# Long convolution by a 64 x 64 transform: sums and differences of n2 and n2+32, products on 64 x 64 quarters, the output inverse with the spectrum stationary

## The chip, the cores and the metric

One core of one Trainium2 chip. The time is that of the device in microseconds, of one execution of the program; shown are the median of three runs and one more execution taken with the profiler. All arithmetic is float32 or split into float32r parts.

## The reference

One encoder layer is applied to two request groups (g = 0, 1) of 2048 tokens and 1024 channels with the same weights:

```
h = rmsnorm(x);  p = h @ w_in                       # 1024 -> 3328 columns
y_hy = x0 * fftconv(v * x1, k2, skip) * silu(z_hy)  # 512 channels
y_cf = conformer(glu(a)) * silu(z_cf)               # 256 channels, 31 taps, LayerNorm
y_xa = attention(q, memory) * silu(z_xa)            # 256 channels, 4 heads, 256 memory tokens
y = rmsnorm(x + concat(y_hy, y_cf, y_xa) @ w_out)
```

`fftconv` is a two-sided long convolution on a circle of 4096 positions, with a filter k2 that a small network computes for each position and channel. The change lies in how this convolution is computed.

## The kernel before, in words

The transform over 4096 positions m = 64 n1 + n2 is done in two steps of 64: over n1 (to a frequency index t of 0 to 63), and over n2. The two request groups are the real and imaginary parts of one complex sequence. Values pass through DRAM between the steps.

The program has four stages:

- **Stage 1** (lines 204 to 707): the projections, 24 TensorE matmuls of 512 columns for each block of 128 output columns and 512 tokens (`proj`, L439 to L441, high and low parts). Beside them run lists of background tasks, some after every block (`background`, L653): the conformer's taps on VectorE (L235), the filter (`filter_background`, L287), and, at the end, the first eight steps of stage A (`a_background`, L613). The filter makes taps for two n2 at a time (`taps`, L330); four quarter products (L355, 64 rows by 64 columns of the array each) transform a pair over n1, two ScalarE copies (L357) evict them, and SyncE stores them to XF (L358). The gated product u = v * x1 is stored to UU for each of 4 channel blocks and 2 groups (L495).
- **Stage A** (`stage_a`, L812, 24 of 32 steps here): for two n2, the input is transposed, split, multiplied by a twiddled table (`times_t1`, L185, six matmuls in row halves), and evicted by one VectorE and one ScalarE copy to X1 (L825 to L828). Two steps go with each block of the memory attention (`attention`, L756, 16 blocks).
- **Stage B** (`stage_b`, L890): for each t of 0 to 32 the filter's row XF[t] is transformed over n2 (`spectrum`, L845: one 128 x 128 product, evicted as two tiles kr and ki of which each half stands twice), then X1[t] and, with a reversed table, X1[64-t] go through `unit` (L831): a 128 x 128 product over n2, two half copies on ScalarE that swap real and imaginary parts, two products with kr and ki, their sum on POOL, the inverse product over n2, an eviction, and a store to AA. Every third t from 9 loads and splits a block of w_out (`wo_load`, L855). The last two blocks of attention each have two steps of stage B behind them; the other steps follow.
- **Output** (lines 922 to 980): for two n2 (128 tokens), AA is loaded, two 64-column products with the table t4 invert over t (L949), ScalarE evicts (L951), four transposes turn channels to partitions (L954), VectorE multiplies by the gate from GG (L958), and 48 float32r matmuls (L972 to L974) multiply by w_out; then residual, norm and store.

A planner orders the instructions of each engine when the program is built, by its own estimate of durations; each engine then executes in that fixed order. DMA issues are instructions of the queue that issues them: loads of stage B and output on SyncE, stores to AA and of the output on ScalarE. A float32 matmul is two instructions on TensorE, a float32r matmul and a transpose one.

Buffers in stages A and B: PSUM `ms` 2, `tr` 3, `pa` 2, `po` 1 banks; SBUF tiles `in` 8, `o` 5, `us` 4, `z` 4, `k0` and `k1` 3 each.

## Time and profile before

| | us |
|---|---|
| median of three runs | 2113.95 (2110.22 to 2114.83) |
| the profiled execution's own time | 2119.94 |
| span from its first to its last instruction | 2118.2 |
| TensorE busy | 1982.9 |
| VectorE, ScalarE, POOL busy | 1262.6, 759.2, 890.4 |

In the profile PE is TensorE, PEld its weight loads, DVE VectorE, ACT ScalarE, SP SyncE; a q behind an engine's name (SPq, ACTq) is its instruction queue, where DMA issues stand. A busy share is an average over the stages, which have different limits; a matmul is pipelined, so the cadence of starts says more than the length of one. A wait is put down to what came last before the instruction started.

### The profile page before, as it was taken

To read this page: it belongs to the slowest core of one execution; us is meant where nothing else is said; L and a number is where in the kernel's file an instruction comes from. 1 tells how busy PE (TensorE), PEld (TensorE's weight loads), DVE (VectorE), ACT (ScalarE), POOL (GpSimd) and SP (SyncE) were. 2 spreads that over 40 slices of the span, in tenths; PEclk is the share of its full clock that TensorE was granted. 3 is DMA by queue.
4 is the path that set the end of the run, shared out by engine and by line. 5 is a ranking of instruction groups with operands and counts; after the bars stand their busy time and mean duration, and the time that the engine had idled before them with its cause. 6 is when DMAs were issued, how large, how long until landed. Compare 5 with 4: busy or idle time off the path is not lost. (4 is left out here: it accounts for less than half of the span.)

```text
span 2118.2 us, 26007 instructions
## 1 busy us (share of the span) xinstructions
PE 1982.9 (94%) x8866; PEld 1499.7 (71%) x8866; DVE 1262.6 (60%) x1779; ACT 759.2 (36%) x1461; POOL 890.4 (42%) x854
## 2 busy tenths in 40 slices
PE   5999988898999999999989999999988889999998
PEld 5888877776777777777767778777533267777776
DVE  4766397979325365488889622178887624434443
ACT  5531122231424233321323421278787722222221
POOL 3433576755533211466645531166588711111110
PEclk8999999999999999999999999999999999999999
DMA  9643323332557423232422235698888785555552
GB/s 335 209 145 130 94 87 96 120 119 80 203 182 220 137 89 115 81 95 65 124 69 94 87 107 173 221 288 269 246 264 257 235 219 140 147 155 151 154 144 60
DMA packets 238558, 328.72 MB, mean 155 GB/s; under 512 B 87177, under 2 KB 117913, under 8 KB 236634
## 3 DMA queue, kind: packets, MB, share of 16 engines
q1 hardware_dynamic: 146026, 260.72, 38.7%
q10 hardware_dynamic: 87056, 54.57, 9.6%
q0 software_dynamic: 5344, 11.77, 2.1%
q8 instruction: 71, 1.16, 0.2%
q14 instruction: 61, 0.50, 0.1%
HBM read 196.37 MB, written 130.61 MB: 154 GB/s over the span
## 5 line engine op out<-in xcount | busy, mean ns | idle before, releaser
L439 PE MATMUL pj<-xh,whi 128*128 128x512 f32 (+1 forms) x1728 | 671.1, 389 | 32.1 <-ACT big L505 9.3
L440 PE MATMUL pj<-xl,whi 128*128 128x512 f32 (+1 forms) x1728 | 670.1, 388 | 8.6 <-POOL xl L410 6.6
L441 PE MATMUL pj<-xh,wlo 128*128 128x512 f32 (+1 forms) x1728 | 668.7, 387 | 0.0
L235 DVE SCALAR_TENSOR_TENSOR bg<-bg,vb,bg 128x512 f32<-128x512 f32 x480 | 415.3, 899 | 11.4 <-POOL bg L230 7.0
L439 PEld LDWEIGHTS pj<-xh,whi 128*128 128x128 f32 x1728 | 331.6, 192 | 101.5 <-ACT big L505 11.0
L440 PEld LDWEIGHTS pj<-xl,whi 128*128 128x128 f32 x1728 | 332.1, 192 | 74.2 <-POOL xl L410 7.5
L441 PEld LDWEIGHTS pj<-xh,wlo 128*128 128x128 f32 x1728 | 332.0, 192 | 66.3 <-issue 2.2
L972 PE MATMUL ms<-wo,mh 128*128 128x512 f32 x512 | 204.2, 399 | 2.2 <-ACT mh L193 2.2
L973 PE MATMUL ms<-wo,mh 128*128 128x512 f32 x512 | 201.3, 393 | 0.0
L974 PE MATMUL ms<-wo,ml 128*128 128x512 f32 x512 | 194.3, 397 | 0.2 <-POOL ml L194 0.2
L462 DVE SCALAR_TENSOR_TENSOR sm<-sm,va,sm 128x448 f32<-128x448 f32 (+1 forms) x96 | 84.2, 877 | 162.4 <-POOL sm L460 143.0
L460 POOL TENSOR_SCALAR sm<-sm,va 128x448 f32<-128x448 f32 (+1 forms) x96 | 119.9, 1249 | 120.0 <-ACT sm L453 112.7
L481 POOL TENSOR_TENSOR big<-big,sm 128x448 f32<-128x448 f32 (+1 forms) x64 | 121.7, 1904 | 112.1 <-DVE sm L464 108.7
L975 DVE TENSOR_TENSOR xr<-xr,ms 128x512 f32<-128x512 f32 x64 | 44.0, 688 | 199.2 <-PE ms L974 199.0
L200 POOL TENSOR_TENSOR ss<-ss,mhalf 128x1 f32<-128x1 f32 x32 | 17.7, 553 | 313.3 <-DVE ss L199 313.3
L453 ACT COPY sm<-pj 128x512 f32<-128x512 f32 x96 | 56.2, 586 | 222.0 <-PE pj L441 189.6
L972 PEld LDWEIGHTS ms<-wo,mh 128*128 128x128 f32 x512 | 96.9, 189 | 47.5 <-issue 24.3
L974 PEld LDWEIGHTS ms<-wo,ml 128*128 128x128 f32 x512 | 96.6, 189 | 20.9 <-DVE mf L958 0.8
L973 PEld LDWEIGHTS ms<-wo,mh 128*128 128x128 f32 x512 | 96.9, 189 | 20.0
L194 POOL TENSOR_TENSOR wlo<-sm,whi 128x512 fp32r<-128x512 f32 x50 | 79.5, 1603 | 63.2 <-ACT whi L193 37.0
L198 ACT ACTIVATE junk<-xr 128x1024 bf16<-128x1024 f32 x32 | 33.8, 1058 | 191.4 <-DVE xr L975 191.4
L840 POOL TENSOR_TENSOR z<-z,us 128x512 f32<-128x512 f32 x64 | 81.9, 1289 | 28.0 <-DVE us L839 21.9
(174 smaller groups left out, 2784.2 us busy)
## 6 DMA issues: line engine op xcount, KB each, us to landing
big<-in_xt_dram SPq DMA_DIRECT2D x32, 512.0 KB, 5.4
in<-x1d SPq DMA_DIRECT2D x128, 128.0 KB, 3.9
aa<-o ACTq DMA_DIRECT2D x64, 256.0 KB, 3.6
at<-aa SPq DMA_DIRECT2D x64, 256.0 KB, 5.1
out_dram<-xr ACTq DMA_DIRECT2D x64, 256.0 KB, 3.7
sm<-in_win_dram SPq DMA_DIRECT2D x52, 256.0 KB, 3.2
ws<-whi SPq DMA_DIRECT2D x52, 256.0 KB, 2.3
ws<-wlo SPq DMA_DIRECT2D x52, 256.0 KB, 2.2
```

Source lines behind the costliest of these rows:

```text
L194: (sub_eng or nc.gpsimd).tensor_tensor(lo, src, hi.bitcast(F32), op=ALU.subtract)
L235: nc.vector.scalar_tensor_tensor(st["a", c], st["h", c][:, k:k + TB], vb[:, 2 * k + c:2 * k + c + 1], st["a", c], op0=ALU.mult, op1=ALU.add)
L439: nc.tensor.matmul(ps[:, ts_], hi, xh[:, k, ts_], start=k == 0, stop=False)
L440: nc.tensor.matmul(ps[:, ts_], hi, xl[:, k, ts_], start=False, stop=False)
L441: nc.tensor.matmul(ps[:, ts_], lo, xh[:, k, ts_], start=False, stop=k == KC - 1)
L460: nc.gpsimd.tensor_scalar(ct[:, o:e], pt[:, o + 1:e + 1], w[1], va[:, 52 + ch:53 + ch], op0=ALU.mult, op1=ALU.add)
L462: nc.vector.scalar_tensor_tensor(ct[:, o:e], pt[:, o:e], w[0], ct[:, o:e], op0=ALU.mult, op1=ALU.add)
L481: nc.gpsimd.tensor_tensor(v, v, out, op=ALU.mult)
L840: nc.gpsimd.tensor_tensor(z, z, us, op=op)
L972: nc.tensor.matmul(po, mh[:, k, :], woh[k][:, hs], start=i == 0, stop=False)
L973: nc.tensor.matmul(po, mh[:, k, :], wol[k][:, hs], start=False, stop=False)
L974: nc.tensor.matmul(po, ml[:, k, :], woh[k][:, hs], start=False, stop=i == 7)
```

## The change

The 64 values of n2 are put in the order 0, 32, 1, 33, ... so that a pair is n2 and n2+32. Where a pair is evicted (filter, `a_background`, `stage_a`), `butterfly` stores its sum and its difference: ScalarE evicts one bank, VectorE adds and subtracts. The transform over n2 then falls into one over 32 sums (even frequencies) and one over 32 differences (odd frequencies), each with real and imaginary part a 64 x 64 table, so that four such products fill the four quarters of the array.

`stage_b` takes t and 64-t together in 32 steps (t = 0 with 32): one group of four quarters transforms both, two groups make the spectrum kr and ki for both (for t = 0 four full products with a table `sk`), VectorE makes four products of them, and two groups, accumulated in PSUM, make the inverse, whose tables carry the combination of real and imaginary products. Two ScalarE copies fill one tile, and two stores of 64 rows of 4 KB go to AA. Six loads of 128 KB and two stores of 256 KB per step, as before for a pair.

The output inverse multiplies with AA's tile as the stationary operand and the table t4 (now 128 columns, for both tokens of a pair) as the moving one, eight products of 128 columns; the result has channels on partitions already. Its 128 tokens are those of n2 = n and n+32. The gate's loads become four of 64 elements a row for two of 128; the gate's product is one VectorE instruction for two. The store to UU is issued in two halves.

```diff
@@ butterfly, new; filter_background @@
+    def butterfly(a, b, px):
+        nc.scalar.copy(b, px[1])
+        nc.vector.tensor_tensor(a, px[0], b, op=ALU.add)
+        nc.vector.tensor_tensor(b, px[0], b, op=ALU.subtract)
...
+                butterfly(st["f", 0], st["f", 1], px)
                 for q in range(2):
-                    nc.scalar.copy(st["f", q], px[q])
                     nc.sync.dma_start(XF[n2p // 2, q * P:(q + 1) * P, :], st["f", q])
@@ hy_u @@
-                    nc.scalar.dma_start(UU[i].rearrange("c (n g t) -> c n g t", g=2, t=32)[:, :, g, :],
-                                        st["u"].rearrange("p (n t) -> p n t", t=32))
+                    for q in range(2):
+                        nc.scalar.dma_start(UU[i].rearrange("c (n q g t) -> c n q g t", q=2, g=2, t=32)[:, :, q, g, :],
+                                            st["u"][:, q * 1024:(q + 1) * 1024].rearrange("p (n t) -> p n t", t=32))
@@ stages A and B: psum, tiles, stage_a (a_background alike) @@
-        ms, tr, pa, po_ = psum(c2, ms=2, tr=3, pa=2, po=1)
+        ms, tr, pa = psum(c2, ms=2, tr=4, pa=2)
...
-            return tl_("in", 8)
+            return tl_("in", 7)
...
-            return tl_("o", 5)
+            return tl_("y", 2)
...
-            o = po_()
+            o = tr()
...
             times_t1(px, th, tl, uh, ul)
+            xo = tl_("z", 6), tl_("z", 6)
+            butterfly(*xo, px)
             for s in range(2):
-                xo = tl_("us", 4)
-                (nc.scalar.copy if s else nc.vector.tensor_copy)(xo, px[s])
-                nc.scalar.dma_start(X1[2 * n + s, 0:128, :], xo)
+                nc.scalar.dma_start(X1[2 * n + s, 0:128, :], xo[s])
@@ stage_b; unit, spectrum, fetch and stage_b of before are gone @@
+        lo_, hi_ = slice(0, 64), slice(64, 128)
+        def quarters(banks, jobs):
+            n = len(jobs[0][3])
+            for j in range(n):
+                for b, c, r, ops in jobs:
+                    w, x = ops[j]
+                    nc.tensor.matmul(banks[b][c, :], w[r, :], x[r, :], start=j == 0, stop=j == n - 1)
+        def spectrum(t):
+            xf = t_in()
...
+            for j in range(2):
+                pk = ms(), ms()
...
+                    w = stab[:, 2 + j, :]
+                    quarters(pk, [(0, lo_, lo_, [(w, xf)]), (0, hi_, lo_, [(w, xf)]),
+                                  (1, lo_, hi_, [(w, xf)]), (1, hi_, hi_, [(w, xf)])])
+                for b in range(2):
+                    ks.append(tl_("k", 6))
+                    nc.scalar.copy(ks[-1], pk[b])
+            return ks[0:2], ks[2:4]
...
+        def stage_b(t):
+            t1_ = 64 - t if t else 32
+            xa, xb = fetch(t, (0, 1)), fetch(t1_, (1, 0))
+            u = tr(), tr()
+            w0, w1 = stab[:, 0, :], stab[:, 1, :]
+            quarters(u, [(0, lo_, lo_, [(w0, xa)]), (0, hi_, lo_, [(w1, xb)]),
+                         (1, hi_, hi_, [(w0, xa)]), (1, lo_, hi_, [(w1, xb)])])
+            kr, ki = spectrum(t)
+            z = [[None, None], [None, None]]
+            for j, k in enumerate((kr, ki)):
+                for b in range(2):
+                    z[j][b] = tl_("z", 6)
+                    nc.vector.tensor_tensor(z[j][b], u[b], k[b], op=ALU.mult)
+            o = pa(), pa()
+            quarters(o, [(h, c, r, [(stab[:, 4 + 2 * v + j, :], z[j][b]) for j in range(2)])
+                         for h, c, r, v, b in ((0, lo_, lo_, 0, 0), (0, hi_, lo_, 1, 1),
+                                               (1, lo_, hi_, 0, 1), (1, hi_, hi_, 1, 0))])
+            om = tl_("o", 2, 1024)
+            for h in range(2):
+                nc.scalar.copy(om[:, h * TB:(h + 1) * TB], o[h])
+            for k, r in ((t, lo_), (t1_, hi_)):
+                nc.scalar.dma_start(AA[k, 0:64, :], om[r, :])
+            if t >= 9 and t % 3 == 0:
+                wo_load(t // 3 - 3)
@@ output @@
-        ms, tr = psum(c3, ms=4, tr=4)
+        ms, tr = psum(c3, ms=5, tr=3)
...
                 for g in range(2):
-                    nc.sync.dma_start(g8[:, :, g, :], chans(GG, g, n))
+                    for q in range(2):
+                        nc.sync.dma_start(g8[:, :, g, q, :], chans(GG, g, q, n))
...
-            yt = tr()
-            for s in range(2):
-                nc.tensor.matmul(yt[64 * s:64 * s + 64, :], t4[:, 2 * i + s, :], at[:, s, :], start=True, stop=True)
-            ys = sp.tile([P, TB], F32, tag="ys", name=nm("ys"))
-            nc.scalar.copy(ys, yt)
             yc = tr()
             for k in range(4):
-                nc.tensor.transpose(yc[:, k * P:(k + 1) * P], ys[:, k * P:(k + 1) * P], ident)
+                for h in range(2):
+                    nc.tensor.matmul(yc[:, k * P:(k + 1) * P], at[:, h, k * P:(k + 1) * P], t4[:, i, h, :],
+                                     start=h == 0, stop=h == 1)
```

## Rows read from the trace of the kernel before

**Rows 1.** The page, busy time, share and instructions; VectorE's busy tenths in 40 slices.

```profile
PE 1982.9 (94%) x8866; PEld 1499.7 (71%) x8866; DVE 1262.6 (60%) x1779; ACT 759.2 (36%) x1461; POOL 890.4 (42%) x854
...
DVE  4766397979325365488889622178887624434443
```

**Rows 2.** Busy us (instructions) by stage: PE, PEld, DVE, ACT, POOL; clock, DMA share, GB/s.

```profile
930.00:1200.00 270.00, 247.74 (x1060) 189.31 (x1059) 229.74 (x295) 83.11 (x118) 147.09 (x144) 0.99 0.29 86
...
1400.00:1490.00 90.00, 90.00 (x676) 64.41 (x676) 73.59 (x149) 71.63 (x237) 54.99 (x69) 1.00 0.84 264
...
1530.00:1694.00 164.00, 141.03 (x289) 51.92 (x287) 122.90 (x172) 125.05 (x219) 134.54 (x105) 0.96 0.80 254
...
1710.00:2000.00 290.00, 289.51 (x1278) 218.30 (x1279) 113.81 (x160) 64.94 (x116) 42.35 (x46) 0.99 0.60 157
```

**Rows 3.** The same, a stretch of 30 us in stage 1.

```profile
960.00:990.00 30.00, 26.57 (x116) 21.40 (x116) 30.00 (x41) 4.70 (x8) 16.02 (x16) 1.00 0.34 73
```

**Rows 4.** Groups by line, whole run: busy us, mean ns | idle before, releasers.

```profile
L840 POOL TENSOR_TENSOR z<-z,us 128x512 f32<-128x512 f32 x64 | 81.9, 1289 | 28.0 <-DVE us L839 21.9 <-DVE z L838 1.6 <-PE ms L847 1.5
...
L838 DVE TENSOR_TENSOR z<-tr,k 128x512 f32<-128x512 f32 x64 | 43.9, 689 | 23.2 <-ACT us L836 17.1 <-POOL z L840 2.7 <-issue 1.3
...
L842 PEld LDWEIGHTS pa<-z,stab 128*128 128x128 f32 x128 | 23.1, 196 | 46.1 <-POOL z L840 28.6 <-issue 15.8 <-POOL us L839 0.9
```

**Rows 5.** Line 357: duration ns min/median/max, first and last start.

```profile
L357 ACT COPY f<-ms x32: 564/589/595, 775.1 to 1236.7; 128x512 f32<-128x512 f32 x32
```

**Rows 6.** Waits, 900 to 1200 us: us in total, times, longest.

```profile
ACT f L357 <- PE ms L355: 25.8, 5, 7.5
...
PEld ms L355 <- DVE f L341: 10.5, 10, 2.5
...
ACT L340 <- DMA xf<-f: 6.2, 4, 3.2
```

**Rows 7.** Line 828, the stores of stage A: duration ns, first and last start.

```profile
L828 ACTq DMA_DIRECT2D x1d<-us x48: 326/326/1031, 1389.2 to 1491.6; - x48
```

**Rows 8.** DMA, 1530 to 1690 us: the sum, and the stores to AA with landing time.

```profile
DMA packets 23461, 41.20 MB, mean 258 GB/s; under 512 B 3737, under 2 KB 3737, under 8 KB 23336
...
aa<-o ACTq DMA_DIRECT2D x58, 256.0 KB, 3.5
```

**Rows 9.** Timeline of PE in stage B: start us, us, instruction, count.

```profile
1601.10 0.59 PE L842 MATMUL pa<-z,stab 128*128 128x512 f32 x1
1601.53 1.88 PE L833 MATMUL tr<-in,stab 128*128 128x512 f32 x4
```

**Rows 10.** Timeline of PE and PEld around one group of four quarter products.

```profile
784.26 0.21 PEld L355 LDWEIGHTS ms<-f,f 64*64 64x64 f32 x8 [0.35 <-issue]
784.26 1.09 PE L355 MATMUL ms<-f,f 64*64 64x512 f32 x8
...
785.28 0.48 PE L310 MATMUL ms<-f,wf 66*128 66x256 f32 x1
```

**Rows 11.** Timeline of PE in the output, from before L949 to after it.

```profile
1901.34 0.39 PE L974 MATMUL ms<-wo,ml 128*128 128x512 f32 x1
...
1903.00 0.39 PE L973 MATMUL ms<-wo,mh 128*128 128x512 f32 x1
```

**Rows 12.** Timeline of PE in the output, around the transposes.

```profile
1908.69 0.39 PE L973 MATMUL ms<-wo,mh 128*128 128x512 f32 x1
1908.92 0.39 PE L974 MATMUL ms<-wo,ml 128*128 128x512 f32 x1
...
1909.82 0.40 PE L972 MATMUL ms<-wo,mh 128*128 128x512 f32 x1
```

**Rows 13.** Timeline of PE in stage 1, around products of 128 columns.

```profile
66.05 0.61 PE L388 MATMUL ms<-bg,ones 128*128 128x128 f32 x4
66.41 0.36 PE L439 MATMUL pj<-xh,whi 128*128 128x256 f32 x1
66.61 0.28 PE L440 MATMUL pj<-xl,whi 128*128 128x256 f32 x1
```

More of the change, by code (lines that the diff above doesn't have):

```diff
@@ L94, in _tables, with forward @@
-    fr = (4 * np.arange(16)[:, None, None] + np.arange(2)[None, :, None] + 2 * np.arange(2)).reshape(-1)
-    fr = np.concatenate([fr, 64 + fr])
-    sf = s2(cp, sp)[fr]
-    kz, kh = kz[fr], kh[fr]
-    stab = np.stack([s2(cp, sp), s2(cpr, spr), s3(cp.T, sp.T), s3(cpr.T, spr.T), kz, kh, sf], axis=1)
+    jj, ab, pair = np.arange(32), np.arange(32)[:, None], np.arange(2)
+    def forward(k2, conj=1.0):
+        th = 2 * np.pi * ((ab * k2[None, :]) % 64) / 64
+        w = np.zeros((32, 2, 2, 32))
+        w[:, 0, 0], w[:, 1, 0] = np.cos(th), np.sin(th)
+        w[:, 0, 1], w[:, 1, 1] = -conj * np.sin(th), conj * np.cos(th)
+        return w.reshape(64, 64)
@@ new lines, in inverse, with both @@
+    def inverse(k2, conj, turned):
+        th = 2 * np.pi * ((k2[:, None] * ab.T) % 64) / 64
+        w = np.zeros((2, 32, 2, 32))
+        re = np.stack([np.cos(th), np.sin(th)], axis=1)
+        im = conj * np.stack([-np.sin(th), np.cos(th)], axis=1)
+        w[0], w[1] = (im, -re) if turned else (re, im)
+        return w.reshape(64, 64)
+    def both(a, b):
+        return np.concatenate([a, b], axis=0)
+    ev, od, evr, odr = 2 * jj, 2 * jj + 1, 62 - 2 * jj, 63 - 2 * jj
+    fk = both(forward(ev), forward(od))
@@ new lines, in _tables @@
+    kr, ki = np.tile(fk[:, :32], 2), np.tile(fk[:, 32:], 2)
+    stab = np.stack([both(forward(ev), forward(od)), both(forward(odr, -1.0), forward(evr, -1.0)), kr, ki] + [
+        both(inverse(ev, 1.0, u), inverse(od, 1.0, u)) for u in (False, True)] + [
+        both(inverse(evr, -1.0, u), inverse(odr, -1.0, u)) for u in (False, True)], axis=1)
+    sk = np.zeros((2, 32, 2, 4, 2, 2, 32))
+    for h in range(2):
+        k2 = 2 * jj + h
+        th, al = 2 * np.pi * ab * k2 / 64, np.pi * ab / 64 + 2 * np.pi * ab * k2 / 64
+        sg = (-1.0) ** h
+        g0, g1 = (np.cos(al), -np.sin(al)), (-sg * np.sin(al), -sg * np.cos(al))
+        for c_ in range(2):
+            for v in range(2):
+                sk[h, :, 0, 2 * c_ + h, h, v] = (np.cos(th), -np.sin(th))[c_]
+                sk[0, :, 1, 2 * c_ + h, 1 - h, v] = (g0[c_] + g1[c_]) / 2
+                sk[1, :, 1, 2 * c_ + h, 1 - h, v] = (g0[c_] - g1[c_]) / 2
@@ L131 @@
     X1 = dram.tile([64, 129, 512], F32, name="x1d")
-    AA = dram.tile([64, 129, 512], F32, name="aa")
+    AA = dram.tile([64, 65, 1024], F32, name="aa")
     const = ctx.enter_context(tc.tile_pool(name="const", bufs=1))
@@ L824, in stage_a @@
             times_t1(px, th, tl, uh, ul)
+            xo = tl_("z", 6), tl_("z", 6)
+            butterfly(*xo, px)
             for s in range(2):
[L826 to L843 removed]
@@ L845, in spectrum @@
-        def spectrum(x, t):
-            pk = ms()
-            nc.tensor.matmul(pk, stab[:, t, :], x, start=True, stop=True)
-            kr, ki = tl_("k0", 3), tl_("k1", 3)
-            nc.vector.tensor_copy(kr[0:64, :], pk[0:64, :])
-            nc.vector.tensor_copy(kr[64:128, :], pk[0:64, :])
-            nc.scalar.activation(ki[0:64, :], pk[64:128, :], AF.Copy, scale=-1.0)
-            nc.vector.tensor_copy(ki[64:128, :], pk[64:128, :])
-            return kr, ki
+                nc.scalar.dma_start(X1[2 * n + s, 0:128, :], xo[s])
@@ new lines @@
+        lo_, hi_ = slice(0, 64), slice(64, 128)
[7 more added lines that the diff above has]
+            xf = t_in()
+            src = XF[:, 0:256, :].rearrange("m (h e k) c -> m h e k c", h=2, e=4)
+            for h, r in enumerate((lo_, hi_)):
+                nc.sync.dma_start(xf[r, :], src[:, h, :, t, :])
+            if t == 0:
+                sk = t_in().rearrange("p (j c) -> p j c", j=4)
+                nc.sync.dma_start(sk, a["sk"])
+            ks = []
+            for j in range(2):
+                pk = ms(), ms()
+                if t == 0:
+                    for b in range(2):
+                        nc.tensor.matmul(pk[b], sk[:, 2 * j + b, :], xf, start=True, stop=True)
+                else:
+                    w = stab[:, 2 + j, :]
[5 more added lines that the diff above has]
+            return ks[0:2], ks[2:4]
@@ new lines, in fetch @@
+        def fetch(t, order):
+            x = t_in()
+            src = X1[:, 0:128, :].rearrange("(n h) (r k) c -> n h r k c", h=2, r=2)
+            for h, r in zip(order, (lo_, hi_)):
+                nc.sync.dma_start(x[r, :], src[:, h, :, t, :])
+            return x
+        def stage_b(t):
[8 more added lines that the diff above has]
+            for j, k in enumerate((kr, ki)):
+                for b in range(2):
+                    z[j][b] = tl_("z", 6)
[5 more added lines that the diff above has]
+            om = tl_("o", 2, 1024)
+            for h in range(2):
+                nc.scalar.copy(om[:, h * TB:(h + 1) * TB], o[h])
[3 more added lines that the diff above has]
+                wo_load(t // 3 - 3)
@@ L886, in more_a @@
                     na += 1
[L888 removed]
+        stab = sp.tile([P, 8, 64], F32, name="stab", bufs=1)
         nc.sync.dma_start(stab, a["stab"])
[L890 to L902 removed]
         na, nb = LEAD, 0
```

100 lines of the change are left out of this document (26 added, 74 removed).

## The prediction

> **What bounds the kernel now.** I read the page first, for engine shares and slices; then busy time by stage, since the change works in four stages with different limits; then the waits, the groups by line, and the timeline where a price had to be read off. TensorE is busy for 94% of the span, VectorE for 60%, but VectorE comes in stretches at nine tenths [rows 1]. By stage [rows 2]: in 930 to 1200 us (projections with the filter and the conformer taps beside them) TensorE still has 22 us without work, while VectorE is busy for 230 of 270 us; one 30 us stretch of it is full, 30.00 of 30 [rows 3], and two like it stand at 1050 and 1140. In 1400 to 1490 (attention with stage A) TensorE has no gap and VectorE is at 82%. In 1530 to 1694 (stage B) four engines lie between 75% and 86% and the DMA share is 0.80: no single resource, but a round of work over all of them. In 1710 to 2000 (output) only TensorE counts, 289.5 of 290.
>
> **Stage 1, the filter's pairs.** Of a pair of taps two ScalarE evictions stood after the four quarter products; now it is one eviction, a VectorE sum and a VectorE difference. The price is that of a product that reads one PSUM and one SBUF operand, 0.69 us [rows 4]: 16 pairs put 22 us on VectorE and take 16 x 0.59 = 9 us off ScalarE [rows 5]. Pairs come at about one in 29 us (32 evictions from 775 to 1237 [rows 5]), so some 9 fall into 930 to 1200, 9 x 1.38 = 13 us. Its free time there is 40 us, but not in the full stretches, where what it runs late TensorE waits for (the quarter products on the taps' product, 10.5 us) [rows 6]. A wait is added too: the sum on VectorE now waits for the eviction, which already waits for TensorE in its own order (25.8 us in 5 times) [rows 6]; queued behind it on VectorE are the conformer taps and the short convolutions, and behind those the release of SBUF for TensorE's evictions. SyncE's store of the pair goes out some 1.4 us later, and ScalarE's next exponential, which waits for that store (6.2 us now) [rows 6], a little longer. Bounds: 0 (all in free time) and +13 (all in full stretches). I take **+5**. The eight pairs of stage A at the end of stage 1 and the second DMA issue of each of the eight stores of the gated product cost nothing: VectorE and ScalarE are mostly idle after 1200, and ScalarE's evictions there wait for TensorE.
>
> **Stage A beside attention.** 24 times one more VectorE operation of 0.69 us: 16.6 us, with ScalarE's count unchanged. 48 stores, so 24 steps, start between 1389.2 and 1491.6 [rows 7]: 4.45 us a step, 8.9 us a block of attention with two of them. VectorE is busy for 73.6 of 90 us, 0.82 x 8.9 = 7.3 per block, and goes to 7.3 + 1.4 = 8.7: it fits barely. If VectorE holds no more than nine tenths of its time, the block is 9.7 us, and twelve blocks cost +9. Bounds 0 and +12 (one us a block, for sums that come late to the X1 stores); I take **+4**, nearer the sum that fits. The second buffer for the silu(z) tile instead of five is enough: its load has a whole block to land. SBUF and PSUM regroupings otherwise cost nothing: the counts per block stay.
>
> **Stage B.** Before, a frequency pair took 5.52 us: 58 stores in the 160 us from 1530, two per pair [rows 8], so 29 pairs there. Removed per pair: four half-tile copies and a negation on ScalarE, three copies and a VectorE product, and all of POOL's work (two combinations of 1.29 us and a product), for which the weight loads of the last product waited 28.6 us [rows 4]. Added: four evictions of the spectrum on ScalarE and four VectorE products of 0.69. So VectorE falls to 2.8 us per pair, POOL to the split of w_out alone, ScalarE to six evictions, 3.5 us, with two DMA issues.
> TensorE does not fall. Before, five full products of two instructions at 0.43 us, the distance of their starts [rows 9]: 4.3 us. Afterwards five groups of four quarters. One such group stands in the trace: eight instructions from 784.26, the next work at 785.28, 1.02 us [rows 10], so the four quarters do run together. Its first pass carries its own weight load, and the next instruction has another shape; between groups of one shape neither need be, which would give 0.86. Five groups: 4.3 to 5.1 us.
> In the same rows all eight weight loads are issued within 0.21 us of 784.26, so those of the second pass lie beside running first passes in all four quarters [rows 10]; I therefore take 0.9 per group, 4.5 us. The Trainium skill (TensorE: Matmul & The Clock Gate, Part 3, The mechanism) has a weight load overlap a running matmul only where its row group differs; by that rule no load hides behind a full set of quarters, and the sum would go by the upper figure. The rows speak against it.
> A new ring: the spectrum's two halves share two PSUM banks, so the second half's products wait for both evictions of the first. A group's 1.09 us [rows 10] and two evictions of 0.59 make 2.27 us, twice per pair 4.5 us; queued behind these evictions on ScalarE are the output evictions and the DMA issues.
> The bytes stay: 1.31 MB per pair in six loads on SyncE and two stores on ScalarE, now 4 KB rows for the stores, at 258 GB/s over the stretch [rows 8]. At 4.5 us a pair they alone would be 291 GB/s, so DMA is not excluded as the bound: at the rate of before nothing is gained. Bounds: -30 (29 x (5.52 - 4.5)) and 0. TensorE and the ring at 4.5 each with the slack that such rounds need, I take 5.0: 29 x 0.52 = **-15**.
>
> **Output.** Removed per step: two 64-column products, which stretch two plain steps of 0.23 from 1901.34 to 1903.00, so 1.66 - 0.46 = 1.20 us [rows 11], and four transposes, which stretch two such steps to 0.90: 0.44 [rows 12]; also a ScalarE eviction that nobody waits long for. Added: eight products of 128 columns in two instructions each. The same shape stands in the norm: four instructions from 66.05 to 66.41, and 0.20 from the narrow one behind them to its successor [rows 13]: between 0.36/4 = 0.09 and 0.56/4 = 0.14 each. I take 0.11, nearer the row without the follower: 16 x 0.11 = 1.76, net 0.12 x 32 = +4, with bounds of (1.44 - 1.64) x 32 = -6 and (2.24 - 1.64) x 32 = +19; at the start the first token step is an eviction shorter, -1. The gate loads become four of 256-byte rows for two of 512, on SyncE, with 0.60 of the DMA in use [rows 2]: hidden, and if not, a load of some 4 us late once in 25 us would show. **+3**.
>
> **Sum**: 5 + 4 - 15 + 3 = -3 us on the profiled execution's 2119.94 us (span 2118.2). That run stands 0.3% above the median of 2113.95, so about 2111 us. A measurement of this kernel tells 0.2%, 4 us, from no change.
>
> **Rivals.** (a) Stage B runs at its floors: POOL and the half-tile copies were what stretched the round, and the ring hides behind other products. For it: TensorE waits for POOL in before; against it: the DMA rate it needs. 4.5 us a pair, and stages 1 and A at 2 each: 2 + 2 - 30 + 3 = -23, 2091 us. (b) **Slower, VectorE becomes the bound** where it was nearly that: 13 in stage 1 and 9 in stage A, with stage B at 5.2 (-9) and output at +5: +18, 2132. It decides once VectorE passes nine tenths of a block of attention, 8.0 of 8.9 us, and it is at 7.3 before. (c) Weight loads do not hide in the quarters: 5.1 us of TensorE, 5.5 with slack, so stage B gains nothing, 5 + 4 + 0 + 3 = +12, 2126. The rows of the group speak against it; it is what the skill's rule above would make of it. (d) The change doesn't do what it says: the quarters run one after another, or the granted clock falls from the 2.4 to the 1.2 GHz level in stage B. Five groups take 8.6 us or more, 29 x 3.1 = +90; the granted clock there is 0.96 now and the quarter group ran at full rate.
>
> **Chances.** The forecast, 2103 to 2119 us as its own range, 0.42 (0.16 of it more than 0.2% faster, 0.18 within, 0.08 slower); (a) 0.26, with a small part, 0.03, within 0.2%; (b) 0.22, of which 0.03 ends within 0.2%; (c) 0.08; (d) 0.02. Faster 0.16 + 0.23 = 0.39, within 0.2% 0.18 + 0.03 + 0.03 = 0.24, slower the rest, 0.37. The range of 2090 to 2134 takes in most of (a) and (b) and all of (c).
>
> **What would show it.** Stage B: stores of two rows each 5.0 us, POOL busy only with w_out, six ScalarE evictions per pair; groups of quarters 0.9 us apart where nothing waits. Stage A: blocks still about 9 us with VectorE near full; longer blocks mean (b). Stage 1: TensorE's waits for the filter's quarter products longer than 10.5 us. Output: steps of 12.7 us for 12.6, eight 128-column products at 0.22 each. Wrong would be a pair of 5.5 us with DMA at its share of before, or full stretches of VectorE that reach past 1200.

## The result, and the profile after

| | before | after |
|---|---|---|
| median, us | 2113.99 (2110.22 to 2114.83) | 2200.97 (2198.76 to 2203.90) |
| ratio, 95% interval | | 1.0413 [1.0400, 1.0426] |
| span of the profiled execution | 2118.2 | 2202.1 |

The change makes the kernel 4% slower; the forecast was 2111 us, its range 2090 to 2134. The profiled span grew by 84 us. The first and last DMA issues of each stage say where. First the stores of the filter and of stage A, the last product of attention's blocks and the stores of stage B, by source line (durations in ns, first and last start; the store lines answer to [rows 7] and [rows 8]):

```profile
L386 SPq DMA_DIRECT2D xf<-f x32: 319/320/712, 785.3 to 1266.1; - x32
...
L823 DVE TENSOR_TENSOR ynp<-tr,y x10: 680/692/693, 1426.6 to 1524.5; 128x512 f32<-128x512 f32 x10
...
L857 ACTq DMA_DIRECT2D x1d<-z x48: 326/327/1494, 1400.5 to 1530.3; - x48
...
L925 ACTq DMA_DIRECT2D aa<-o x58: 452/530/1127, 1601.4 to 1775.9; - x58
```

and of before, the same product of nine blocks and the stores of t to AA:

```profile
L794 DVE TENSOR_TENSOR ynp<-po,o x9: 691/692/692, 1417.4 to 1489.0; 128x512 f32<-128x512 f32 x9
L895 ACTq DMA_DIRECT2D aa<-o x31: 326/326/399, 1532.0 to 1694.9; - x31
```

- **Stage 1:** stage A's first store comes at 1400.5 us instead of 1389.2 [rows 7]: +11.
- **Stage A:** its 48 stores take 129.8 us instead of 102.4: +27. Ten blocks of attention end between 1426.6 and 1524.5, 10.88 us each; nine of before ended between 1417.4 and 1489.0, 8.95 each.
- **Stage B:** from the last x1d store to the last aa store (1694.9 before) it takes 245.6 us instead of 203.3: +42. The steady part is 29 pairs at 6.12 us (174.5 us over 28.5 pairs) instead of 5.52 [rows 8], so +17. The rest, +25, lies between stage A's last store and the steady pace. (Counted from store to store as after, the pair of before is 5.43: 61 stores from 1532.0 to 1694.9; the two parts are then +20 and +22.)
- **Output:** 426.2 us instead of 423.3: +3.

The busy time by stage, columns as in [rows 2] (PE, PEld, DVE, ACT, POOL; clock, DMA share, GB/s):

```profile
930.00:1200.00 270.00, 252.77 (x1058) 193.46 (x1058) 241.07 (x304) 78.01 (x110) 151.65 (x145) 0.96 0.30 89
...
1400.00:1530.00 130.00, 128.41 (x811) 88.22 (x810) 103.05 (x201) 84.55 (x280) 66.59 (x81) 1.00 0.72 217
...
1600.00:1776.00 176.00, 154.69 (x1102) 62.40 (x1095) 72.94 (x111) 99.47 (x184) 20.18 (x16) 0.98 0.73 223
...
1790.00:2080.00 290.00, 288.52 (x1447) 245.11 (x1448) 106.61 (x135) 62.73 (x90) 55.17 (x45) 0.99 0.66 162
```

In stage A VectorE is at 79%, below the 82% of [rows 2], so it is not what fills the stage. TensorE is nearly full there (128.4 of 130 us), with 811 instructions in 130 us where it had 676 in 90. In stage B every engine but TensorE is less busy than before and the DMA share fell from 0.80 to 0.73; TensorE is at 88%. I read that as a round in which the engines wait for each other in turn.

**What fills TensorE in stage A.** Its timeline, from one run of the row halves of `times_t1` to the next:

```profile
1440.15 0.49 PE L212 MATMUL pa<-r,th 64*128 64x512 f32 x1
1440.48 0.39 PE L212 MATMUL pa<-r,tl 64*128 64x512 f32 x1
1440.71 0.39 PE L212 MATMUL pa<-r,th 64*128 64x512 f32 x1
1441.04 1.08 PE L821 MATMUL tr<-ynp,wo 128*64 128x256 f32 x8
...
1443.51 0.50 PE L212 MATMUL pa<-r,th 64*128 64x512 f32 x1
```

and the same in the kernel before, where the line is L190:

```profile
1435.74 0.50 PE L190 MATMUL pa<-k,th 64*128 64x512 f32 x2
1436.08 0.40 PE L190 MATMUL pa<-k,tl 64*128 64x512 f32 x2
1436.32 0.39 PE L190 MATMUL pa<-k,th 64*128 64x512 f32 x2
1436.64 0.66 PE L785 MATMUL tr<-ident,ynp 128*128 128x128 f32 x4
```

Before, the two halves of the array worked at once: six matmuls in 0.90 us. Now three matmuls of one half take 0.89 us, then other work follows, and the three of the other half take another 0.9. So it is in 22 of these 24 steps; before, 22 of 24 had the six together. A block has two steps: 4 x 0.89 instead of 2 x 0.90 us, +1.76 us of TensorE's time beside the 1.93 by which a block grew. How much of the growth it explains only experiments 3 and 5 show. Nothing in the source line changed; the planner put other work between the halves. The bank px[1] comes free after ScalarE's copy, px[0] only after VectorE's difference, so one half is ready for its next step earlier than the other; experiment 3 tests this.

**What the round in stage B is.** ScalarE's timeline over one pair, with ACTq its store issues:

```profile
1648.75 1.07 ACT L923 COPY o<-pa 128x512 f32<-128x512 f32 x2 [0.71 <-PE pa L871]
1649.85 1.12 ACTq L925 DMA_DIRECT2D aa<-o  x2
1651.07 1.07 ACT L893 COPY k<-ms 128x512 f32<-128x512 f32 x2 [1.25 <-issue]
1652.83 1.07 ACT L893 COPY k<-ms 128x512 f32<-128x512 f32 x2 [0.69 <-PE ms L871]
1654.62 1.07 ACT L923 COPY o<-pa 128x512 f32<-128x512 f32 x2 [0.71 <-PE pa L871]
```

and the waits in 1600 to 1776 us (total, times, longest):

```profile
DVE z L916 <- ACT k L893: 100.7, 70, 3.0
PEld ms L871 <- ACT k L893: 53.7, 73, 1.8
ACT k L893 <- PE ms L871: 24.9, 34, 1.4
```

From output copies to output copies it is 5.87 us. I read it as a closed loop: copies of the output 1.07, issue of the two stores 1.12, spectrum copies 1.07, a wait of 0.69 while TensorE refills the two spectrum banks, spectrum copies 1.07, a wait of 0.71 for the inverse, and some 0.14 between them. Experiment 8 tests it. VectorE and TensorE wait for the spectrum copies; those stand behind the store issues. The issues are not counted as busy, so the page shows ScalarE at 57%. One issue (64 rows of 4 KB) takes 530 ns in the median; those of before (128 rows of 2 KB) took 326 ns on the same engine.

### The profile page after: what moved, and what is told of

Its sections match the earlier page's. It is cut to its first block, busy times and chain, and to the rows that moved or that the text cites. A ratio compares the mean times of both kernels' runs of the same rounds, so it can differ in the third digit from the quotient of the medians.

```text
span 2202.1 us, 28057 instructions
## 1 busy us (share of the span) xinstructions
PE 2054.4 (93%) x10072; PEld 1574.9 (72%) x10072; DVE 1230.6 (56%) x1743; ACT 730.5 (33%) x1385; POOL 780.9 (35%) x759
## 4 chain that ended last, share of the span: by engine, by line
PE 63%; DVE 16%; DMA 7%; issue 4%; ACT 4%; POOL 3%; ACTq 2%; SPq 1%; POOLq 0%; DVEq 0%
PE pj L467 10%; PE pj L468 10%; PE pj L469 10%; DVE bg L263 10%; PE ms L1017 5%; PE ms L1018 5%; PE ms L1019 5%; PE tr L1000 3%; PE ms L871 2%; PE pa L212 2%; DVE sm L490 2%; PE pa L871 2%; PE ms L799 1%; PE tr L814 1%; PE tr L821 1%
## 5 line engine op out<-in xcount | busy, mean ns | idle before, releaser
L467 PE MATMUL pj<-xh,whi 128*128 128x512 f32 (+1 forms) x1728 | 677.9, 393 | 41.6 <-ACT big L534 16.4
L916 DVE TENSOR_TENSOR z<-tr,k 128x512 f32<-128x512 f32 x128 | 84.5, 688 | 118.2 <-ACT k L893 113.4
L871 PE MATMUL ms<-in,stab 64*64 64x512 f32 x496 | 119.7, 632 | 17.6 <-ACT k L893 17.6
L871 PE MATMUL pa<-z,stab 64*64 64x512 f32 x512 | 122.4, 621 | 2.0 <-DVE z L916 2.0
L1017 PEld LDWEIGHTS ms<-wo,mh 128*128 128x128 f32 x512 | 97.6, 191 | 22.0 <-ACT mh L221 4.3
```

The source lines that it names most:

```text
L467: nc.tensor.matmul(ps[:, ts_], hi, xh[:, k, ts_], start=k == 0, stop=False)
L871: nc.tensor.matmul(banks[b][c, :], w[r, :], x[r, :], start=j == 0, stop=j == n - 1)
L916: nc.vector.tensor_tensor(z[j][b], u[b], k[b], op=ALU.mult)
L1017: nc.tensor.matmul(po, mh[:, k, :], woh[k][:, hs], start=i == 0, stop=False)
```

## The experiments

In all of them the kernel before ran on the same chip; its medians lay between 2114.9 and 2116.9 us. "The pair" is stage B's steady pace. Theory 1 (in stage B the wave theory): the planner takes apart row halves and quarters that would run together, and TensorE is filled by the pieces. Its rivals: VectorE's and ScalarE's work on the sums in stage A, and in stage B the ring through the two spectrum banks (the ring theory). Theory 3, on ScalarE's store issues, came only with experiment 7.

**1. Hold the halves together** (`times_t1`; each matmul is held behind the one before it on TensorE):

```diff
-                nc.tensor.matmul(px[s], w[r, :], u[r, :], start=j == 0, stop=j == 2)
+                mm = nc.tensor.matmul(px[s], w[r, :], u[r, :], start=j == 0, stop=j == 2)
+                if s or j:
+                    tc.keep_in_program_order(mm)
```

> Theory 1: stage A lost time because the planner sets other instructions between the two row halves of a step of times_t1, so that the halves run one after another. Here each of the six matmuls is held behind the one before it on TensorE, so most halves stand next to each other again. Expected: the attention block falls from 10.93 us to 9.0 to 9.4 us, the x1d stores of stage A take 106 to 112 us instead of 129.8, the kernel 2177 to 2185 us. Rival: the blocks are long because of the sum and difference on VectorE and the copy in front of them; then the block stays at 10.7 to 11 us and the kernel at 2196 to 2206 us. Stage B keeps its 5.9 to 6.1 us a pair either way.

Measured: 2194.5 us, 1.0376 [1.0334, 1.0419]; 10.6 us a block (six ends from 1468.5 to 1521.4). A miss for both sides: the block fell by 0.3 us, but stage A's stores took 135.9 us instead of 129.8, and the interval overlaps that of the changed kernel, so no gain is shown. The hold fixes the order and not the distance: in 22 of 24 steps the planner still set other work between the first matmul and the other five.

**2. Hold the quarters together** in stage B (the same hold in `quarters`, jobs of the bank released last first).

> Theory 1 for stage B: the four quarters of a group run together only if the planner leaves them side by side. Here the quarters of the bank that comes free last go first and each quarter is held behind the one before it. Expected: most waves hold four quarters, the pair of stage B falls from 6.1 us to 5.2 to 5.5 us, the kernel 2176 to 2186 us; stage A keeps its 10.9 us a block. Rival: the pair is set by the ring through the two spectrum banks (TensorE fills a bank, ScalarE copies it, VectorE multiplies); then the pair stays at 5.9 to 6.1 us although the quarters stand together, and the kernel at 2196 to 2206 us.

Measured: 2199.8 us, 1.0406 [1.0375, 1.0437]; 58 stores from 1600.0 to 1780.2 us, 6.32 us a pair. In its timeline most quarters stand in full sets of four, and nothing was gained: split groups do not set stage B's pace.

**3. Let both banks come free together** (px and o each one tile of two banks, nothing held):

```diff
-        ms, tr, pa = psum(c2, ms=2, tr=4, pa=2)
+        ms, tr = psum(c2, ms=2, tr=4)
+        pap = c2.enter_context(tc.tile_pool(reuse_waits="tile", name=nm("pspa"), bufs=1, space=PS))
+        def pa_pair():
+            t = pap.tile([P, 2, TB], F32, tag="pa", name=nm("pa"))
+            return t[:, 0, :], t[:, 1, :]
...
-            px = pa(), pa()
+            px = pa_pair()
...
-            o = pa(), pa()
+            o = pa_pair()
```

> Only the banks px and o of stages A and B are changed: the two banks are one tile, so that both come free at the same time; nothing is pinned. Theory 1 says that the planner splits a pair because one bank of it is ready earlier: the halves of times_t1 then stand together by themselves, the attention block falls to 9.0 to 9.4 us, stage B gains little (its transform and spectrum groups are still split), and the kernel takes 2174 to 2186 us. Rival (evictions): sharing one release makes the wait for the subtraction bind both banks, so the block stays at 10.9 us or grows, and the kernel takes 2200 to 2215 us.

Measured: 2185.3 us, 1.0327 [1.0290, 1.0364]. The halves ran together again by themselves, in all 24 steps, which shows why they had been apart:

```profile
1460.10 0.50 PE L212 MATMUL pa<-r,th 64*128 64x512 f32 x2
1460.44 0.39 PE L212 MATMUL pa<-r,tl 64*128 64x512 f32 x2
1460.67 0.39 PE L212 MATMUL pa<-r,th 64*128 64x512 f32 x2
1461.00 0.73 PE L805 MATMUL ms<-wo,wo 128*128 128x256 f32 x4
...
1464.13 0.63 PE L820 MATMUL tr<-ident,ynp 128*128 128x128 f32 x4 [0.36 <-DVE ynp L829]
```

The six matmuls are back at 0.90 us, but the block fell only to 10.5 us (seven ends from 1452.1 to 1514.9), not to 9.0 to 9.4, and stage A's stores still took 131.0 us. TensorE now has gaps: of its 4.4 us of waits in 1440 to 1500 us some are at transposes (last row above), and the largest, 2.0 us, is that of these matmuls for the difference, which now frees both banks:

```profile
PE pa L212 <- DVE z L218: 2.0, 4, 0.6
```

Why the halves stood apart is shown; of the 1.76 us that this takes of TensorE in a block, 0.4 came back in the block. The rival of this run, that one release makes the wait for the difference bind both banks, is there too.

**4. Both orders held and shared banks:**

> Both orders held and px and o each one tile of two banks. Theory 1: blocks at 9.0 to 9.4 us, pairs of stage B at 5.2 to 5.5 us, the kernel 2150 to 2165 us, some 36 to 50 us below the changed kernel. Rival (VectorE and ScalarE around the sums, and the ring of the spectrum): under 10 us of gain, 2190 to 2205 us.

Measured: 2185.0 us, 1.0332 [1.0308, 1.0357], the same as shared banks alone. This was against theory 1 as the whole story, and stage B's part of it fell.

**5. The rest of stage A's loss.** On the kernel of 3, plain copies in place of the sums:

```diff
-            butterfly(*xo, px)
+            nc.vector.tensor_copy(xo[0], px[0])
+            nc.scalar.copy(xo[1], px[1])
```

> As the kernel with shared banks, but in stage A the two results go out by plain copies, one on VectorE and one on ScalarE (this leaves out the sum and difference for most of the x1d rows). If the rest of the lost time in stage A (10.2 us a block against 8.95 us) lies in the sum, the difference and the copy that both wait for, the block falls to 8.9 to 9.3 us and the kernel to 2162 to 2174 us. If it lies in the attention's output sharing the four tr banks, the block stays at 10.0 to 10.4 us and the kernel at 2180 to 2190 us.

Measured: 2182.0 us, 1.0312 [1.0277, 1.0347]; a block 9.66 us (eight ends from 1437.3 to 1504.9). This kernel leaves out the sum and the difference in stage A. They, with the copy that both wait for, are 0.8 of the remaining 1.5 us a block, and stage A's stores fall from 131.0 to 113.4 us. The other 0.7 is not they. The kernel as a whole did not gain against that of 3: stage B took 246.4 us instead of 226.0. It is not the shared tr bank either: with attention's output in a bank of its own (`psum(c2, ms=2, tr=3, po=1)`)

> As the kernel with shared banks, but attention's output has a bank of its own again and tr three (the transform in stage B then has one and a half pairs). If the shared tr banks hold back the transposes, the block falls from 10.2 to 8.9 to 9.4 us; if the sum and difference are the rest, it stays at 10.0 to 10.4 us. Stage B can only lose by it, by 0 to 1.5 us a pair; so the kernel takes 2165 to 2215 us and the block decides.

the block stayed at 10.3 us, while stage B with three tr banks went to 8.3 us a pair and the kernel to 2246.4 us, 1.0619 [1.0595, 1.0643].

Steady blocks leave out that attention can run ahead of stage A. So count from stage A's first store until both its last store and the last product of attention's fourteenth block have started (the early pairs of stage B come behind it): 114.3 us before (1389.2 to 1503.5), 140.2 after the change (1400.5 to 1540.7), 131.0 with shared banks (1401.8 to 1532.8), 123.3 with the copies on top (1403.2 to 1526.5). Of the 26 us, joined halves give back 9, the sums 8, and 9 are neither. The rows that end these four, in this order:

```profile
L794 DVE TENSOR_TENSOR ynp<-po,o x14: 680/692/692, 1389.3 to 1503.5; 128x512 f32<-128x512 f32 x14
L823 DVE TENSOR_TENSOR ynp<-tr,y x14: 680/692/693, 1406.7 to 1540.7; 128x512 f32<-128x512 f32 x14
L863 ACTq DMA_DIRECT2D x1d<-z x48: 326/326/722, 1401.8 to 1532.8; - x48
L829 DVE TENSOR_TENSOR ynp<-tr,y x14: 677/678/692, 1408.5 to 1526.5; 128x512 f32<-128x512 f32 x14
```

**6. Stage B behind attention** (`if n >= 14: more_b(2)` left out):

> Only the early start of stage B is taken back: its pairs are planned behind the last block of attention. Theory: the first pairs wait for their loads in TensorE's order and hold up attention's last two blocks, which end at 1555 and 1588 us; without it they end at about 1538 to 1545 us, stage B is in its steady pace by 1575 us instead of 1600 us, and the kernel takes 2180 to 2192 us. Rival: the start is the latency of the loads and the filling of the banks, whatever stands before it: 2197 to 2210 us.

Measured: 2189.3 us, 1.0348 [1.0331, 1.0365]. Attention's last block ended at 1555.0 instead of 1587.6 us and the steady pace began at 1565. So 12 us of the 25 at the start came from the early pairs, which stand ahead of attention's products in TensorE's order. In 1530 to 1600 us of the changed kernel TensorE's longest waits are 3.1 us for the load of sk, 2.8 for a spectrum copy and 2.3 for a load of X1.

The granted clock comes on top: in that window its mean is 0.82 in the changed kernel and 0.98 here. From the end of the wait of 2.8 us on, the changed kernel's TensorE ran at the lower level, 1.2 GHz, for 20 us:

```profile
1564.00:1584.50 20.50, 18.46 (x62) 8.15 (x66) 5.22 (x11) 8.43 (x24) 4.12 (x4) 0.50 0.25 66
```

That belongs to this execution more than to the change. The two kernels of experiment 11 have the same stages A and B; their clock in the window is 0.93 and 0.98 and their stage B took 239.0 and 242.6 us instead of 245.6. On the kernel of 4:

> The kernel with both orders held and shared banks, and stage B planned behind attention. If the two gains (16 us and 12 us) are of different causes, they add: 2168 to 2177 us. If the shared banks had already taken away the delay at the start, it stays at 2180 to 2188 us.

Measured: 2179.9 us, 1.0303 [1.0285, 1.0322]. The two gains overlap in part: 21 us of 16 + 12.

**7. The ring of the spectrum.** One of each two spectrum copies to VectorE (`(nc.vector.tensor_copy if b else nc.scalar.copy)(ks[-1], pk[b])`), in the changed kernel and in that of 4:

> Stage B alone: of the two spectrum copies of each half, the second goes to VectorE, so the two banks come free together half a microsecond sooner, twice a pair. Ring theory (TensorE fills the two spectrum banks, ScalarE copies both, only then may TensorE fill them again): the pair falls from 6.1 us by 0.5 to 1.1 us, the kernel from 2201 to 2168 to 2186 us, though the quarters are as split as before. Wave theory (split groups of quarters fill TensorE): the pair stays within 0.2 us, the kernel at 2195 to 2206 us. Stage A keeps its 10.9 us a block.

> As the kernel with both orders held and shared banks, where TensorE's order is the same to the instruction; only the second of each two spectrum copies goes to VectorE, so that the two banks come free together. In the earlier run of this edit alone the planner took the groups apart in other places, so it told nothing apart. Ring theory: the pair falls from 5.9 us to 4.9 to 5.4 us, the kernel from 2185 to 2158 to 2172 us. Rival (the loads of the pairs, or TensorE's own time, set the pace): the pair stays at 5.7 to 6.0 us, the kernel at 2180 to 2192 us.

Measured: 2201.5 us, 1.0402 [1.0375, 1.0428], and 2186.7 us, 1.0344 [1.0323, 1.0365]: no gain in either. In the second ScalarE's two waits of a pair are 1.28 and 1.06 us where the kernel of 4 has 1.18 and 0.19, so nearly the 1.07 of copies that it was spared came back as waits; VectorE makes its copy and its products one after the other, and the issue of the stores stands where it stood:

```profile
1655.58 0.59 ACT L905 COPY k<-ms 128x512 f32<-128x512 f32 x1 [1.28 <-PE ms L880]
1657.22 1.07 ACT L935 COPY o<-pa 128x512 f32<-128x512 f32 x2 [1.06 <-PE pa L880]
```

With the second half's copies, and so the imaginary spectrum, left out altogether (`for b in range(2 - 2 * j)`)

> As the kernel with both orders held and shared banks, but the second half of the spectrum is multiplied out on TensorE and not copied: its products with the transform use the first half's copies (this leaves out the imaginary spectrum). TensorE's work and all transfers stay. Ring theory: one of two round trips from TensorE to ScalarE and back is gone, the pair falls from 5.9 us to 4.3 to 5.1 us, the kernel to 2150 to 2168 us. Rival (loads): the pair stays at 5.7 to 6.0 us, the kernel at 2180 to 2192 us. Rival (TensorE is full): likewise.

the kernel took 2262.4 us, 1.0699 [1.0679, 1.0718], against every theory. The planner ordered the groups anew, ScalarE's output copies waited 71.3 of 130 us with spectrum products as the last thing done before them, and TensorE's mean granted clock was 0.87; it tells nothing apart. What these runs had in common was in ScalarE's timeline: the store issues ahead of the spectrum copies. That is theory 3.

**8. The stores off ScalarE's queue** (`nc.gpsimd.dma_start(AA[k, 0:64, :], om[r, :])`):

> Only the stores of stage B's results are issued from GpSimd's queue instead of ScalarE's. Theory 3: in the steady pace ScalarE's stream is one closed loop of 5.86 us (output copies 1.07, issue of two stores 1.1 to 1.3, spectrum copies 1.07, wait 0.7, spectrum copies 1.07, wait 0.7), and the issue stands in it between the output copies and the copies for which TensorE waits. Without it the pair falls by 0.6 to 1.2 us to 4.8 to 5.4 us, the kernel from 2201 to 2165 to 2183 us, with the quarters as split as before. If TensorE's waves or the loads set the pace, the pair stays at 5.8 to 6.0 us and the kernel at 2195 to 2206 us.

Measured: 2195.2 us, 1.0369 [1.0347, 1.0391]. Plain pairs fell from 5.87 to 5.0 us (stores at 1595.2, 1600.2, 1605.2, 1610.2 us), as theory 3 says, and the kernel gained only 6 us: the pairs that load a part of w_out grew to 7 to 11 us. A new wait had taken the place, in 1610 to 1740 us:

```profile
ACT wo L221 <- DMA in<-in_w_out_dram: 28.6, 11, 5.2
```

The same with orders held, shared banks and stage B behind attention, and with one copy on VectorE beside that:

> Both orders held, shared banks, stage B behind attention, and the stores issued from GpSimd. Theory 3 with the groups together: the pair at 4.6 to 5.2 us, the kernel from 2180 to 2142 to 2160 us. If TensorE's waves bound the pair once the issue is gone, this kernel gains more by the stores than the changed one alone; if the loads bound it, both stop at the same pair.

> The same with the second of each two spectrum copies on VectorE. It gained nothing while ScalarE issued the stores. If the loop through ScalarE still sets the pace without them, another 0.3 to 0.6 us a pair goes, the kernel at 2128 to 2148 us; if TensorE or the loads set it then, within 4 us of the kernel without this edit.

Measured: 2175.2 us, 1.0271 [1.0247, 1.0296], and 2176.6 us, 1.0279 [1.0259, 1.0298]. Plain pairs 4.9 us; sharing the copies gives nothing.

**9. Buffers for w_out.** `in` has seven buffers, a pair takes three and a w_out load two. Here w_out goes into stage A's input buffers, empty by then:

```diff
-            for h in range(2):
-                raw, hs = t_in(), slice(h * TB, (h + 1) * TB)
-                nc.sync.dma_start(raw, a["w_out"][0, k * P:(k + 1) * P, hs])
-                split(woh[k][:, hs], wol[k][:, hs], raw)
+            raw = tl_("u4", 2, 1024)
+            for h in range(2):
+                hs = slice(h * TB, (h + 1) * TB)
+                nc.sync.dma_start(raw[:, hs], a["w_out"][0, k * P:(k + 1) * P, hs])
+                split(woh[k][:, hs], wol[k][:, hs], raw[:, hs])
```

> The kernel with orders held, shared banks, stage B behind attention and stores from GpSimd has plain pairs of 4.9 us, but every third pair, which also loads a part of w_out, takes 7 to 9 us. Here the w_out parts go into the two buffers that stage A used for its input, which are empty in stage B, and no longer into two of the seven in buffers from which a pair takes three. Theory: the w_out loads leave too few in buffers for the next pairs; then the long pairs fall to 5.0 to 6.0 us, stage B from 212 to 187 to 197 us, the kernel from 2175 to 2149 to 2162 us. Rival: the long pairs are the transfers themselves (half a megabyte more) or ScalarE's and GpSimd's work on them; then they stay at 7 us or more and the kernel at 2168 to 2180 us.

Measured: 2153.5 us, 1.0178 [1.0153, 1.0203]; pairs of 4.86 us from 1591 on (a few up to 5.5), the long ones gone, 267 GB/s. Stage B took 198.0 us, 5 less than before the change. TensorE's timeline there:

```profile
1644.99 1.09 PE L880 MATMUL pa<-z,stab 64*64 64x512 f32 x8 [0.23 <-ACT o L935]
1645.90 1.15 PE L880 MATMUL ms<-in,stab 64*64 64x512 f32 x8
1646.76 0.59 PE L880 MATMUL tr<-in,stab 64*64 64x512 f32 x2
```

**10. These two edits alone** on the changed kernel:

> The changed kernel with two edits alone: stage B's stores issued from GpSimd, and the w_out parts loaded into stage A's empty input buffers. No order is held, no bank shared, stage B starts early. If the split groups of quarters cost stage B nothing of their own, the steady pair is 4.9 to 5.1 us as in the kernel with all edits (4.86), stage B takes 205 to 218 us and the kernel 2165 to 2178 us. If they cost once ScalarE's loop is open, the pair is 5.3 us or more and the kernel at 2180 us or above.

Measured: 2170.6 us, 1.0262 [1.0236, 1.0287]. The pair is 4.98 us and TensorE has no gap in 1610 to 1710 us:

```profile
1610.00:1710.00 100.00, 100.00 (x812) 49.82 (x807) 53.51 (x81) 62.91 (x121) 21.22 (x40) 1.00 0.85 265
```

ScalarE's timeline, now without issues between output copies and spectrum copies:

```profile
1641.74 1.08 ACT L923 COPY o<-pa 128x512 f32<-128x512 f32 x2
1642.70 1.10 ACT L893 COPY k<-ms 128x512 f32<-128x512 f32 x2
1644.59 0.59 ACT L893 COPY k<-ms 128x512 f32<-128x512 f32 x1 [0.79 <-PE ms L871]
```

Split groups cost stage B at most about the 0.12 us a pair between 4.98 and 4.86; the two kernels differ in the shared banks and the early pairs too. Of the 30 us that the two edits give back, the stores alone had given 6: their issue hid the shortage of buffers. The buffers alone were not tried.

**11. Stage 1.** Plain copies for the filter's pairs, then for stage 1's own x1d pairs too:

> The changed kernel with the filter's pair in stage 1 sent out by two ScalarE copies, as before the change (this leaves out the sum and difference of the filter's spectrum). If VectorE's two more operations a pair are what stage 1 lost, the last store of the filter's spectrum comes at 1240 to 1250 us instead of 1266, the first x1d store of stage A at 1388 to 1393 instead of 1400, and the kernel takes 2190 to 2194 us. If it is the split upload of the gated input or the x1d pairs made during stage 1, the times stay within 3 us.

> The changed kernel with the filter's pairs and stage 1's own x1d pairs sent out by plain copies as before the change (this leaves out both sums and differences in stage 1). Plain copies of the filter alone gave back 5 of the 11 us. If VectorE's and the banks' later release by the sums are all that stage 1 lost, the first x1d store of stage A comes at 1387 to 1391 us and the kernel takes 2187 to 2191 us; if the gated input's upload in two parts or the planner's order of other work has a share, 1393 to 1397 us and 2193 to 2197 us.

Measured: 2194.7 us, 1.0379 [1.0352, 1.0406], and 2195.5 us, 1.0381 [1.0361, 1.0402]. The last filter store came at 1248.1 us, stage A's first at 1395.8 and 1396.5. These kernels leave out the sums of the filter, then also of stage 1's pairs. In the other runs, which all have stage 1 as changed, stage A's first store lies between 1394.6 and 1404.3, so a single trace does not tell 5 us; the medians of time, 5 to 6 us lower in both runs, and the filter's last store, 1248.1 and 1251.3 where the others have 1261 to 1269, speak for it. So the filter's sums cost some 5 of the 11 us, the x1d pairs nothing that shows, and 6 us are left that are neither; the two-part upload of the gated product and the planner's other order were not tried.

## Why the prediction was wrong

**Stage 1, +5 predicted, +11 measured.** The filter's sums cost some 5, as forecast, and by one of the ways named: ScalarE's exponential waits for the filter's store, in 900 to 1200 us now, and below it with the filter's plain copies of experiment 11:

```profile
ACT L368 <- DMA xf<-f: 19.3, 5, 8.3
...
ACT L368 <- DMA xf<-f: 6.0, 3, 3.2
```

against 6.2 [rows 6]. The other way, and the sign named for it, did not come: TensorE's wait for the quarter products on the taps' product is 7.9 us, not longer than 10.5. The other 6 us, for which the prediction had only "cost nothing", stay open.

**Stage A, +4 predicted, +27 measured.** The step that failed is the price of the sums: VectorE's time alone, "it fits barely", with "SBUF and PSUM regroupings otherwise cost nothing: the counts per block stay". The counts stayed, but the sums free the two banks one after the other. Two row halves cost 0.90 us side by side and 1.78 apart, and whether they stand side by side is the planner's doing; joined again they give back 9 of 26 us (experiment 5). Behind that stands a second limit that the term had not either, TensorE's wait for the sums (2.0 us in 60, experiment 3); without the sums 8 us more come back. The last 9 us stay open. The first part was visible ahead: the trace of before showed pairs (x2), and the eviction was made to free the banks one after the other. Rival (b) had the direction, but not what happened: VectorE has 27 of 130 us free, and TensorE is full.

**Stage B, -15 predicted, +42 measured.** Three terms:
- "I therefore take 0.9 per group" held. In the rows of experiment 9 groups of eight instructions follow each other in 0.91 and 0.86 us. Rival (c) needed 5.1 us of TensorE a pair; the pair of 4.86 us rules it out. The Trainium skill (TensorE: Matmul & The Clock Gate, Part 3, The mechanism) says that a weight load overlaps a running matmul only where its row group differs. The trace does not agree: of groups of 0.86 and 0.91 us two passes at 0.43 leave at most 0.05 us for loads. The same section of the Trainium skill has a load into the background weight buffer pulled ahead too, which would fit; no run here shows that it is this.
- The ring was the step that failed here. It was summed as "a group's 1.09 us and two evictions of 0.59", twice 2.27, and the output evictions and DMA issues were named as queued behind. They are not behind but inside: in ScalarE's timeline the loop is all that stands between one spectrum copy and the same copy of the next pair, 3 x 1.07 of copies, 1.12 of issues and two waits, 5.87 us; with the issues alone taken out of it, plain pairs came to 5.0 (experiment 8). The issue was also no longer 0.33 a store but 0.53. With the issue out and buffers for w_out, the pair is 4.86 to 4.98, the 5.0 that the prediction took.
- The start of stage B had no term at all: +25 us, 12 of them from the early pairs in front of attention's last blocks, by experiment 6. Of the other 13, 3 to 7 did not come again in the kernels of experiment 11, whose granted clock stays higher there; the rest was not settled.

**Output, +3 predicted, +3 measured.** Eight products of two instructions at 0.11 were forecast; the timeline has four in 0.36 and twelve in 1.25, 0.09 and 0.10 each. At that price 16 of them are some 1.6 us for the 1.64 removed, so the term would be about -1 and not the +4 that the sum had. That the number agrees is luck: the +3 is not explained, it stands on one trace of before, and output took 424.1 to 427.5 us in the runs here.

```profile
1907.57 0.60 PE L1000 MATMUL tr<-t,at 128*128 128x128 f32 x4
1907.93 0.48 PE L1017 MATMUL ms<-wo,mh 128*128 128x512 f32 x1
...
1913.47 1.50 PE L1000 MATMUL tr<-t,at 128*128 128x128 f32 x12
1914.72 0.48 PE L1017 MATMUL ms<-wo,mh 128*128 128x512 f32 x1
```

Rival (a), stage B at its floors, would have needed 4.5 us a pair; the best seen is 4.86. Rival (d) came closest in size and not in kind: the quarters do run together, and the granted clock is 0.98 in stage B's steady part.

No version tried beats the kernel before. The best one is 1.0178 of it, and its span of 2154.0 us is 36 longer: +29 in stage A (131.1 us against 102.4 between its first and last store, although its halves run together), +10 ahead of it, +3 in output, -5 in stage B. The transform in quarters pays in stage B, once its loop is open; what stages 1 and A lose beside it is more. The kernel before was not given the same stores and w_out buffers, so how much of the -5 is the transform's is not shown.

## What to carry to other kernels

Where an engine's stream closes a loop with another engine, add up everything that stands in that stream for one round, DMA issues too, although they are not counted as busy; a term "queued behind" can be inside the loop. Two row halves cost 0.90 us here next to each other in TensorE's order and 1.78 with full-array work between them, and banks that came free at different times took them apart: give such banks one release, and look what that release then waits for, since here it gave back a third of the loss. When a stall is removed and the time hardly moves, look for the next wait before dropping the theory: the stores and the w_out buffers together gave 30 us, the stores alone 6.

## What was not expected of the hardware

The issue of a store of 64 rows of 4 KB kept ScalarE's queue for 530 ns in the median and up to 1127, that of 128 rows of 2 KB, the same bytes, for 326; from GpSimd's queue it is 537. And single quarters of different groups overlap too: in the changed kernel one of the inverse, one of the transform and two of the spectrum start between 1646.75 and 1646.81 us, and split groups in stage B cost at most about 0.12 us a pair, while split halves in stage A, with full-array work between them, took 0.89 us each, as much as both take together.
